# Decay broadcasts of a state-space scan on GpSimd's queue, and an output stage whose scalings come later and whose last two pairs stand in source order

## The chip, the cores and the metric

The kernel runs on one core of a Trainium2 chip. The metric is the device time of one execution in microseconds; runs of the kernel before and of a changed kernel are taken on the same chip. Engines are named as the profile names them: PE is TensorE (PEld its weight loads), DVE is VectorE, ACT is ScalarE, POOL is GpSimd and SP is SyncE; a trailing q (ACTq, SPq) marks what an engine's queue issues, such as a DMA.

## The reference, cut to what matters

One layer of a hybrid decoder: a Mamba-2 state-space branch (SSD) and a gated linear attention branch (GLA) work on the same normalized input, are projected, gated and added; the sum goes through an output matrix, is added to the residual stream, and a final RMSNorm ends it. Sequence 2048 and 16 meta tokens ahead of it, width 1024, float32.

```python
def hybrid_layer(hres, norm_w, w_in, ...):
    u = rmsnorm(hres, norm_w)
    proj = jnp.einsum('bld,dn->bln', u, w_in)
    z, xbc, dt_raw, q, k, v, g_gla, a_lr, merge_g = split_cols(proj, IN_WIDTHS)
    xbc = jax.nn.silu(causal_depthwise_conv(xbc, conv_w, conv_b))
    ...
    y_r, _ = ssd_chunked(xs[:, m:], dt[:, m:], a, bm[:, m:], cm[:, m:], SSD_CHUNK, s_m)
    ...
    o_r, _ = gla_chunked(q[:, m:], k[:, m:], v[:, m:], log_a[:, m:], GLA_CHUNK, st_m)
    ...
    branch_proj = jnp.einsum('blnc,ncd->blnd', branches, w_branch)
    gates = jax.nn.sigmoid(merge_g.reshape(b, l, N_BRANCH, D_MODEL))
    merged = jnp.sum(gates * branch_proj, axis=2)
    return hres + jnp.einsum('bld,de->ble', merged, w_out)

def ssd_chunked(x, dt, a, bmat, cmat, chunk, state0):
    da = (dt * a).reshape(b, nc, chunk, h).transpose(0, 3, 1, 2)
    da_cum = jnp.cumsum(da, axis=-1)
    seg = da_cum[..., :, None] - da_cum[..., None, :]
    decay = jnp.exp(jnp.where(causal, seg, -jnp.inf))
    ...

def reference(x, meta_tokens, ...):
    ...
    return rmsnorm(h, final_norm_w)[:, N_META:]
```

## The kernel before, in words

Every large product is made of float32 pairs: a matrix is split into a high and a low part, and `accum` (L187 to L191) issues three matmuls for each pair, high by high, high by low, low by high.

**First stage (to about 1500 us).** The sequence is cut into four blocks of 512 rows. For each block four groups of the SSD branch and four heads of the GLA branch follow each other: `ssd_proj` and `gla_proj` issue the projections on PE, and at each `yield` a `step()` advances the generators that run beside them, `ssd_scan` and `gla_scan` above all. Projections collect in three PSUM banks `pj`; ACT empties a feature's bank with L491 and L492. The first block has 528 columns, which take two banks a feature; the other blocks have 512 and take one. Weights are split into parts by ACT (L169) and POOL (L170) in the first block, stored, and loaded in parts in the later ones. POOL also makes sums of weights and inputs for the second stage (L82), scales the state (L586), copies the ends of the convolution (L494) and takes powers for the norms (L233, L258).

In `ssd_scan` each of the four 128-row chunks of a group needs its cumulated decays as rows, the same on all partitions: four heads by 128 numbers. `fetch_cb` (L507) loads them from the DRAM tile `cumd` with a broadcast DMA of 256 KB into one of three `cb` buffers; `before(c)` fetches chunk c+1 and then reads chunk c with four activations (L569) into `dm`, exponentiates (L571) and masks on DVE (L572); `after(c)`, one step later, uses `dm` on PE (L581). There are 4 blocks x 4 groups x 4 chunks = 64 such DMAs.

**Second stage.** Gates, both branch projections and the output matrix run as stages of a Strassen-like scheme: each pair n of row blocks takes seven products p of 12 matmuls of 512 columns, in the order `PS = (1, 2, 6, 7, 5, 3, 4)` for two pairs in turn. The products accumulate in three kinds of bank, "a" (`pj`), "b" (`pt`) and "c" (`pc`); after products 1, 6 and 5 ACT copies "a" into a snapshot `sn` (L1010). Four of the seven finish a result: `DONE = {2: (0, 0), 5: (1, 1), 4: (1, 0), 3: (0, 1)}` gives the row block i and the column half t. `total` (L1026) adds snapshot and bank on DVE.

**The output stage** is the last one, with eight pairs. Its `use` (L1080) adds the residual half row `r` on DVE (L1084), squares it on ACT with a row sum (L1090), and when both halves of a row are there, makes the mean on DVE (L1092, L1093), the power -1/2 on POOL (L1094), scales both halves by it and by the norm weight `fns` on DVE (L1097), and hands two stores to the next product, where `flush` issues them on ACT's queue (L1164); the last row's go to SP's (L1215). `fetch` (L1071) loads the residual half row two products ahead on SP's queue into one of eight `io` buffers, which the store of a row frees. `load_a` (L965) loads the m tiles on the same queue, `sum_a` (L974 to L977) adds them on POOL, `prep_a` (L983, L984) splits them on ACT and DVE.

**What sets the order.** In the first stage PE and SP keep the order of the source, in the second SP alone; the order of all other instructions of an engine is set by the program's scheduler, which sorts by source order and by readiness in a simulated timeline. `order` lists all products of the second stage, and the functions in `todo` are run at their places in it: `at(pos, fn)` puts fn behind the product with that number.

Of the kernel before, what the change touches and what calls it, by code (L numbers as in the profile page):

```python
# [7 lines left out]
F32 = mybir.dt.float32  # L8
# [34 lines left out]
def trunk_kernel(ctx: ExitStack, tc: tile.TileContext, xm, xmt, w_feat, w_tok, w_zm, w_br, w_o,  # L43
# [462 lines left out]

    def fetch_cb(o, g, c):  # L507
        cbs[g, c] = cb = mk(spool, [P, 4, P], F32, "cb", bufs=3)
        nc.scalar.dma_start(cb, o.cumd[4 * g:4 * g + 4, c * P:(c + 1) * P].unsqueeze(0).to_broadcast([P, 4, P]))

    def ssd_scan(o, g, feats, zs):
        m0, ci0 = o.m0, o.ci0
# [425 lines left out]
    class Stage:  # L938
# [41 lines left out]
        def prep_a(self, n, p):  # L980
            src = self.a[n][p]
            t = mk(apl, [P, 2, 4, P], F32R, "a")
            nc.scalar.activation(t[:, 0], src, AF.Copy)  # L983
            nc.vector.tensor_tensor(t[:, 1], src, t[:, 0].bitcast(F32), op=ALU.subtract)  # L984
            self.a[n][p] = t

        def product(self, n, p, early=False):
            key, pool, tag = {1: ("a", pj, "pj"), 6: ("a",) * 3, 5: ("a",) * 3, 3: ("a",) * 3, 2: ("c", pc, "pc"),
                              7: ("b", pt, "pt"), 4: ("b",) * 3}[p]
            if p in (1, 2, 7):  # L990
                self.ps[n, key] = bank(pool, tag)
            ps = self.ps[n, key]
            a = self.a[n][p]
            for j in range(4):
                bt = self.b[p, j]
                accum(ps, (a[:, 0, j], a[:, 1, j]), (bt[:, 0], bt[:, 1]), p in (1, 2, 7) and j == 0, j == 3,
                      skip_group_check=True)
            if p in (1, 6, 5):
                if early and p == 6:
                    return  # L1000
                self.snapshot(n, p, early)
            if p in DONE:
                key, sn = {2: ("c", 1), 5: ("b", 5), 4: ("b", 6), 3: ("a", None)}[p]
                self.use(n, *DONE[p], self.ps[n, key], self.snap.get((n, sn)))


        def snapshot(self, n, p, early=False):
# [2 lines left out]
            nc.scalar.activation(sn, self.ps[n, "a"], AF.Copy)  # L1010
            self.snap[n, p] = sn

    DONE = {2: (0, 0), 5: (1, 1), 4: (1, 0), 3: (0, 1)}
    stores = []

# [7 lines left out]
    def total(ps, snap):  # L1023
        if snap is None:
            return ps
        nc.vector.tensor_tensor(snap, snap, ps, op=ALU.add)  # L1026
        return snap
# [38 lines left out]
                         "p (k c) -> p k c", c=P), fetch, use)  # L1066

    def out_stage():
        fns, res, ssq = [], {}, {}

        def fetch(n, i, t):  # L1071
            r0 = (2 * n + i) * P
# [4 lines left out]
                    fns.append(mk(opl, [P, BLK], F32, "br", bufs=5))  # L1077
                    nc.sync.dma_start(fns[hf], fnw[:, hf * BLK:(hf + 1) * BLK].to_broadcast([P, BLK]))

        def use(n, i, t, ps, snap):  # L1080
            r0 = (2 * n + i) * P
            r = res[n, i, t]
            x = total(ps, snap)
            nc.vector.scalar_tensor_tensor(r, x, 0.5, r, op0=ALU.mult, op1=ALU.add)  # L1084
            first = (n, i) not in ssq
            if first:
                ssq[n, i] = mk(spl, [P, 2], F32, "ssf")
            q = ssq[n, i]
            jk = mk(spl, [P, BLK], BF16, "junk", bufs=1)
            nc.scalar.activation(jk, r, AF.Square, accum_out=q[:, t:t + 1])  # L1090
            if not first:
                nc.vector.tensor_tensor(q[:, 0:1], q[:, 0:1], q[:, 1:2], op=ALU.add)  # L1092
                nc.vector.tensor_scalar(q[:, 0:1], q[:, 0:1], 1.0 / D, EPS, op0=ALU.mult, op1=ALU.add)  # L1093
                nc.gpsimd.tensor_tensor(q[:, 0:1], q[:, 0:1], mhalf[:, 0:1], op=ALU.pow)  # L1094
                for hf in range(2):
                    o = res[n, i, hf]
                    nc.vector.scalar_tensor_tensor(o, o, q[:, 0:1], fns[hf], op0=ALU.mult, op1=ALU.mult)  # L1097
                    store(out[r0:r0 + P, hf * BLK:(hf + 1) * BLK], o)

        return Stage("out", ("o",), seq // (2 * P),  # L1100
                     lambda n, i, j: m_left[(2 * n + i) // 4][j][:, :, (2 * n + i) % 4 * P:((2 * n + i) % 4 + 1) * P],
                     fetch, use)

    stages = []
    for s in range(nsb):
        stages += [gate_stage(s), branch_stage(s, 0), branch_stage(s, 1)]
# [2 lines left out]

    PS = (1, 2, 6, 7, 5, 3, 4)
    order, begins = [], []
    for st in stages:
        begins.append(len(order))
        for n in range(0, st.npairs, 2):
            ps = PS if (st, n) != (stages[-1], st.npairs - 2) else PS[:5] + (4, 3)
            order += [(st, n + i, p) for p in ps for i in range(2)]
    NEARLY = 6
    AHEAD, LOAD = 5, 9  # L1120
    todo = {}
# [81 lines left out]
    for n in range(2):  # L1203
        st.snapshot(n, 6)

    with tc.manual_schedule(engines={mybir.EngineType.SP}):
        run(-1)
        for i, (st, n, p) in enumerate(order):
            if i >= NEARLY:
                due, stores[:] = stores[:], []  # L1210
                st.product(n, p)
                flush(due)
            run(i)
        for dst, src in stores:
            nc.sync.dma_start(dst, src)  # L1215


def _layout(inputs):
# [83 lines left out]
```

## Time and profile before

| | before |
|---|---|
| median of 3 runs | 2293.7 us (2292.3 to 2297.49) |
| the profiled execution, its own time | 2293.83 us |
| its span, first to last instruction | 2292.0 us |
| PE busy | 2232.7 us (97%) |
| DVE, ACT, POOL busy | 1549.2, 1180.1, 683.8 us |
| mean granted PE clock | 0.994 |
| broadcasts of `cb`, issued on ACT's queue | 64, of 256.0 KB |

The span is what the profiler saw between the first and the last instruction; the execution's own time is 1.83 us longer. A row of the trace gives the start in us from the span's start, the duration, the engine, the line, the operation, output and inputs by name, and how many were merged (x4); a bracket behind it tells how long the engine had sat idle before it and what released it. A row of the list of waits reads: who waited, for whom, total us, times, longest.

### The profile page before, as it was taken

What the parts mean: (1) busy time and instruction counts of PE and PEld (TensorE: products, weight loads), DVE (VectorE), ACT (ScalarE), POOL (GpSimd) and SP (SyncE); (2) the same over time, 40 slices, a digit from 0 to 9 for tenths busy, and PEclk for the clock granted to TensorE, in tenths of its full rate; (3) what the DMA queues carried; (4) which work ended last, traced back from release to release, by engine and by line L of the source; (5) the groups of instructions that cost most, each with busy time, mean ns of one, the idle gap of its engine ahead of it and who ended that gap; (6) DMA issues with size and microseconds to landing.
All of it is one profiled execution on the core that took longest, in us unless ns stands there. A gap on an engine that the chain in (4) does not pass through costs nothing. (4 is left out here: it accounts for less than half of the span.)

```text
span 2292.0 us, 36448 instructions
## 1 busy us (share of the span) xinstructions
PE 2232.7 (97%) x12641; PEld 1944.7 (85%) x12641; DVE 1549.2 (68%) x2895; ACT 1180.1 (51%) x2726; POOL 683.8 (30%) x681
## 2 busy tenths in 40 slices
PE   7899999999999999999999999899999999999997
PEld 6899989888889988888888898778888888788776
DVE  5677676675666676667667666674678845788766
ACT  4665655465534455544455544454544545454443
POOL 3344433122222122211212100066333274323331
PEclk9999999999999999999999999999999999999999
DMA  8766776667787676877667654466768865787743
GB/s 298 234 208 216 272 258 211 219 205 231 245 270 218 221 225 208 264 256 245 206 220 223 219 185 157 130 216 211 234 224 292 300 226 197 245 278 262 244 145 121
DMA packets 301544, 518.04 MB, mean 226 GB/s; under 512 B 27696, under 2 KB 143664, under 8 KB 301360
## 3 DMA queue, kind: packets, MB, share of 16 engines
q1 hardware_dynamic: 200400, 402.84, 54.4%
q10 hardware_dynamic: 100960, 112.88, 14.2%
q8 instruction: 99, 1.62, 0.3%
q14 instruction: 85, 0.70, 0.1%
HBM read 368.42 MB, written 147.19 MB: 225 GB/s over the span
## 5 line engine op out<-in xcount | busy, mean ns | idle before, releaser
L189 PE MATMUL pj<-ue,whl 128*128 128x264 f32 (+1 forms) x672 | 238.8, 355 | 12.3 <-ACT acc L492 6.3
L191 PE MATMUL pj<-ue,whl 128*128 128x264 f32 (+1 forms) x672 | 232.3, 346 | 0.6 <-DVE tkc L399 0.6
L190 PE MATMUL pj<-ue,whl 128*128 128x264 f32 (+1 forms) x672 | 231.3, 344 | 0.0
L189 PE MATMUL pj<-uo,whl 128*128 128x512 f32 x512 | 206.6, 404 | 0.0
L191 PE MATMUL pj<-uo,whl 128*128 128x512 f32 x512 | 200.1, 391 | 0.0
L190 PE MATMUL pj<-uo,whl 128*128 128x512 f32 x512 | 199.4, 389 | 0.0
L82 POOL TENSOR_TENSOR wr<-wr 128x256 f32<-128x256 f32 x80 | 68.5, 857 | 430.6 <-DMA wr<-u 176.2
L189 PE MATMUL pj<-b,a 128*128 128x512 f32 x480 | 189.4, 396 | 6.6 <-ACT sn L1010 5.8
L191 PE MATMUL pj<-b,a 128*128 128x512 f32 x480 | 188.6, 393 | 0.0
L190 PE MATMUL pj<-b,a 128*128 128x512 f32 x480 | 187.8, 391 | 0.7 <-DVE b L959 0.7
L170 POOL TENSOR_TENSOR whl<-wr,whl 128x512 fp32r<-128x512 f32 (+1 forms) x100 | 134.0, 1347 | 181.0 <-ACT whl L169 132.8
L974 POOL TENSOR_TENSOR as<-ar,ar 128x512 f32<-128x512 f32 x40 | 59.1, 1476 | 396.3 <-DMA ar<-in_w_br 114.2
L496 DVE SCALAR_TENSOR_TENSOR acc<-cin,hcw,acc 128x512 f32<-128x512 f32 (+1 forms) x192 | 154.6, 805 | 28.8 <-ACT acc L492 27.9
L984 DVE TENSOR_TENSOR a<-ar,a 128x512 fp32r<-128x512 f32 x160 | 125.5, 793 | 57.0 <-ACT a L983 55.3
L959 DVE TENSOR_TENSOR b<-br,b 128x512 fp32r<-128x512 f32 x140 | 120.5, 877 | 52.6 <-ACT b L958 50.7
L189 PEld LDWEIGHTS pj<-ue,whl 128*128 128x128 f32 x672 | 128.9, 192 | 29.9 <-ACT acc L492 7.4
L189 PE MATMUL pj<-whl,ue 128*128 128x256 f32 (+1 forms) x496 | 144.1, 291 | 2.1 <-ACT ue L315 2.1
L189 PE MATMUL pj<-whl,uo 128*128 128x256 f32 (+1 forms) x496 | 143.3, 289 | 0.6 <-DMA whl<-k_zm 0.6
L191 PEld LDWEIGHTS pj<-ue,whl 128*128 128x128 f32 x672 | 128.9, 192 | 15.8 <-POOL whl L170 0.9
L191 PE MATMUL pj<-whl,ue 128*128 128x256 f32 (+1 forms) x496 | 140.6, 284 | 1.4 <-DVE ue L317 1.4
L190 PEld LDWEIGHTS pj<-ue,whl 128*128 128x128 f32 x672 | 129.1, 192 | 14.8
L191 PE MATMUL pj<-whl,uo 128*128 128x256 f32 (+1 forms) x496 | 140.8, 284 | 0.0
(308 smaller groups left out, 6535.2 us busy)
## 6 DMA issues: line engine op xcount, KB each, us to landing
whl<-k_s SPq DMA_DIRECT2D x96, 512.0 KB, 4.3
whl<-k_g SPq DMA_DIRECT2D x96, 512.0 KB, 4.2
whl<-k_v SPq DMA_DIRECT2D x48, 512.0 KB, 3.8
whl<-k_z SPq DMA_DIRECT2D x36, 512.0 KB, 3.7
wr<-in_w_feat SPq DMA_DIRECT2D x64, 256.0 KB, 4.4
k_s<-whl SPq DMA_DIRECT2D x32, 512.0 KB, 3.7
cb<-cumd ACTq DMA_DIRECT2D x64, 256.0 KB, 5.7
y<-gg ACTq DMA_DIRECT2D x64, 256.0 KB, 4.4
```

Source lines behind the costliest of these rows:

```text
L82: nc.gpsimd.tensor_tensor(o, x, y, op=ALU.subtract)
L170: nc.gpsimd.tensor_tensor(hl[:, 1], raw, hl[:, 0].bitcast(F32), op=ALU.subtract)
L189: nc.tensor.matmul(ps, sh, mh, start=first, stop=False, **kw)
L190: nc.tensor.matmul(ps, sh, ml, start=False, stop=False, **kw)
L191: nc.tensor.matmul(ps, sl, mh, start=False, stop=last, **kw)
L496: nc.vector.scalar_tensor_tensor(acc, cin[:, k:k + tt], hcw[:, ti, k:k + 1], acc, op0=ALU.mult, op1=ALU.add)
L959: nc.vector.tensor_tensor(t[:, 1], raw, t[:, 0].bitcast(F32), op=ALU.subtract)
L974: nc.gpsimd.tensor_tensor(s1, a21, a22, op=ALU.add)
L984: nc.vector.tensor_tensor(t[:, 1], src, t[:, 0].bitcast(F32), op=ALU.subtract)
```

## The change

Three things change. `fetch_cb` issues its DMA from GpSimd's queue instead of ACT's.

In the output stage, for all row blocks but the last four, the mean and the power (`scale`) are issued one product after the row's last product, and the two scalings and stores (`finish`) three products after it, each of them held behind the newest DVE instruction of the source (`behind`, with `latest` set in `use` and `prep_a`).

The last pairs' products stand in source order on PE too (4, 4, 3, 3 at the end, as the list `out_order` has them), and their rows are finished differently: the snapshot is added to `r` ahead of the product's end; the first half row of the last three is multiplied by the norm weight at once; the last product is computed in two halves of 256 columns, each with its own add and square; and the last scalings are shared between ACT and DVE.

```diff
     def fetch_cb(o, g, c):
         cbs[g, c] = cb = mk(spool, [P, 4, P], F32, "cb", bufs=3)
-        nc.scalar.dma_start(cb, o.cumd[4 * g:4 * g + 4, c * P:(c + 1) * P].unsqueeze(0).to_broadcast([P, 4, P]))
+        nc.gpsimd.dma_start(cb, o.cumd[4 * g:4 * g + 4, c * P:(c + 1) * P].unsqueeze(0).to_broadcast([P, 4, P]))
...
             a = self.a[n][p]
+            if (self, n, p) == order[-1]:
+                for c in (slice(0, HB), slice(HB, BLK)):
+                    for j in range(4):
+                        bt = self.b[p, j]
+                        accum(ps[:, c], (a[:, 0, j], a[:, 1, j]), (bt[:, 0, c], bt[:, 1, c]), False, j == 3,
+                              skip_group_check=True)
+                    self.use(n, *DONE[p], ps, None, c)
+                return
...
-        def use(n, i, t, ps, snap):
-            r0 = (2 * n + i) * P
+        def use(n, i, t, ps, snap, cols=None):
             r = res[n, i, t]
-            x = total(ps, snap)
-            nc.vector.scalar_tensor_tensor(r, x, 0.5, r, op0=ALU.mult, op1=ALU.add)
+            if snap is not None and n >= seq // (2 * P) - 2:
+                nc.vector.scalar_tensor_tensor(r, snap, 0.5, r, op0=ALU.mult, op1=ALU.add)
+            else:
+                ps = total(ps, snap)
...
+            c = cols or slice(0, BLK)
+            k = t + (c.start > 0)
+            latest[:] = [nc.vector.scalar_tensor_tensor(r[:, c], ps[:, c], 0.5, r[:, c], op0=ALU.mult, op1=ALU.add)]
+            nc.scalar.activation(jk[:, c], r[:, c], AF.Square, accum_out=q[:, k:k + 1])
+            row = n, i, t
+            if row == at_once[-1] or (first and (n, i) in [w[:2] for w in at_once[1:]]):
+                if k < 2:
+                    nc.vector.tensor_tensor(r[:, c], r[:, c], fns[t][:, c], op=ALU.mult)
+                if k == 1 and not first:
+                    mean(q)
+                if k == 2:
+                    last = nc.vector.scalar_tensor_tensor(q[:, 0:1], q[:, 2:3], 1.0 / D, q[:, 0:1],
+                                                          op0=ALU.mult, op1=ALU.add)
+                    nc.gpsimd.tensor_tensor(q[:, 0:1], q[:, 0:1], mhalf[:, 0:1], op=ALU.pow)
+                    with tc.issue_after(last.ins):
+                        nc.vector.tensor_tensor(r[:, c], r[:, c], fns[t][:, c], op=ALU.mult)
+                    finish(*row)
+            elif row in at_once:
+                scale(*row)
+                finish(*row)
...
+        def finish(n, i, t):
+            r0 = (2 * n + i) * P
+            q = ssq[n, i][:, 0:1]
+            early, late = res[n, i, 1 - t], res[n, i, t]
+            if (n, i, t) in at_once[1:]:
+                nc.scalar.activation(early, early, AF.Identity, scale=q)
+                if (n, i, t) == at_once[-1]:
+                    nc.vector.tensor_scalar(late, late, q, None, op0=ALU.mult)
+                else:
+                    nc.vector.scalar_tensor_tensor(late, late, q, fns[t], op0=ALU.mult, op1=ALU.mult)
+            else:
+                for o, fn in ((early, fns[1 - t]), (late, fns[t])):
+                    nc.vector.scalar_tensor_tensor(o, o, q, fn, op0=ALU.mult, op1=ALU.mult)
+            for hf, o in ((1 - t, early), (t, late)):
+                store(out[r0:r0 + P, hf * BLK:(hf + 1) * BLK], o)
+
+        def behind(fn, *row):
+            with tc.issue_after(latest[0].ins):
+                fn(*row)
+
+        for i, (n, p) in enumerate(out_order):
+            row = n, *DONE.get(p, (0, 0))
+            if p in (3, 4) and i + 4 < len(out_order):
+                later.append((i + 1, lambda row=row: behind(scale, *row)))
+                later.append((i + 3, lambda row=row: behind(finish, *row)))
+            elif p in (3, 4):
+                at_once.append(row)
...
+    for i, fn in later:
+        at(begins[-1] + i, fn)
...
-    with tc.manual_schedule(engines={mybir.EngineType.SP}):
-        run(-1)
-        for i, (st, n, p) in enumerate(order):
...
+    run_out = ExitStack()
+    run_out.enter_context(tc.manual_schedule(engines={mybir.EngineType.SP}))
+    run(-1)
+    for i, (st, n, p) in enumerate(order):
+        if i == len(order) - 2 * len(PS):
+            run_out.close()
+            run_out.enter_context(tc.manual_schedule(engines={mybir.EngineType.PE, mybir.EngineType.SP}))
```

`scale` and `mean` hold the same DVE and POOL instructions as L1092 to L1094. The row sums `ssf` get eight buffers of three columns instead of four of two.

More of the change, by code (lines that the diff above doesn't have):

```diff
@@ L1011, in snapshot @@
             self.snap[n, p] = sn
+    latest, later, order = [], [], []
     DONE = {2: (0, 0), 5: (1, 1), 4: (1, 0), 3: (0, 1)}
@@ L1085, in use @@
             first = (n, i) not in ssq
             if first:
-                ssq[n, i] = mk(spl, [P, 2], F32, "ssf")
+                ssq[n, i] = mk(spl, [P, 3], F32, "ssf", bufs=8)
             q = ssq[n, i]
             jk = mk(spl, [P, BLK], BF16, "junk", bufs=1)
[L1090 to L1098, printed above, removed]
+            c = cols or slice(0, BLK)
```

38 lines of the change are left out of this document (24 added, 14 removed).

## The prediction

> **What bounds the kernel now.** I read the busy line first, then the idle time of PE stretch by stretch, then the list of PE's waits in the two places that the change touches.
>
> ```profile
> span 2292.0 us, 36448 instructions
> PE 2232.7 (97%) x12641; PEld 1944.7 (85%) x12641; DVE 1549.2 (68%) x2895; ACT 1180.1 (51%) x2726; POOL 683.8 (30%) x681
> ...
> 0.00:100.00 100.00, 80.67 (x557) 76.71 (x558) 55.70 (x111) 56.45 (x130) 36.69 (x40) 0.95 0.83 277
> 400.00:1130.00 730.00, 727.52 (x4466) 648.73 (x4464) 478.74 (x1064) 368.54 (x945) 161.72 (x220) 1.00 0.73 231
> 2250.00:2292.00 42.00, 30.55 (x134) 24.69 (x132) 23.39 (x43) 12.53 (x28) 3.24 (x6) 0.90 0.32 111
> ...
> PE pj L189 <- ACT acc L492: 6.3, 5, 4.2
> ...
> PE pj L189 <- ACT sn L1010: 3.8, 3, 2.4
> ```
>
> PE bounds the whole: it is idle for 59.3 us of 2292.0. No matmul is removed, so the change can only win idle time of PE, or lose some. Idle time lies at the two ends: 19.3 us in the first 100 us and 11.4 in the last 42, against 2.5 us in the 730 from 400 on (the first number after the length of a stretch is PE's busy time). The two waits are those that the change can reach: ACT's late emptying of projection banks in the first block (6.3 us, five times), and ACT's late snapshots in the output stage (3.8 us, three times, between 2130 and the end).
>
> **The decay broadcasts.** All 64 leave ACT's queue for POOL's. On ACT they cost nothing now: 1.26 us are four activations 0.29 apart, so that a group begun at 140.46 hands over at 141.63, with the issue of 0.37 us run beside it.
>
> ```profile
> L509 ACTq DMA_DIRECT2D cb<-cumd x64: 361/377/1278, 58.6 to 1318.2; - x64
>   ACT sq L569: 6.5, 8
> ...
> 140.30 0.37 ACTq L509 DMA_DIRECT2D cb<-cumd  x1
> 140.46 1.26 ACT L569 ACTIVATE sq<-cb,tkc 128x128 f32<-128x128 f32 x4
> 141.63 0.97 ACT L569 ACTIVATE sq<-cb,tkc 128x128 f32<-128x128 f32 x3
> 145.55 1.28 ACT L569 ACTIVATE sq<-cb,tkc 128x128 f32<-128x128 f32 x4 [0.71 <-DMA cb<-cumd]
> 147.61 0.59 PE L189 MATMUL pj<-ue,whl 128*128 128x264 f32 x1 [4.17 <-ACT acc L492]
> 195.87 0.39 PE L189 MATMUL pj<-ue,whl 128*128 128x264 f32 x1 [0.71 <-ACT acc L492]
> 143.93 1.26 POOL L170 TENSOR_TENSOR whl<-wr,whl 128x512 fp32r<-128x512 f32 x1 [3.37 <-issue]
> ```
>
> There are three cb buffers and four chunks a group. So three broadcasts of a group are issued with the group before, long ahead, and only the fourth waits for chunk 0 to be read: issued at 140.30, used at 145.55, with ACT already waiting 0.71 us for it. This fourth one is where lateness shows. In two groups of the first block ACT's next work is L491 and L492, which empty the bank that PE waits for (until 147.61 and 195.87, for 4.17 and 0.71 us). Whatever the fourth broadcast loses there, PE loses.
>
> What a broadcast costs on POOL no row shows, nor how much later it lands. From below: zero, the same landing. From above: one op of POOL to write it out and one POOL op already ahead of it in order, 2 x 1.26 = 2.6 us. I take one such op, 1.3 us, since POOL's software handling of 256 KB is nearest to a POOL op of that size (L170). That gives 2 x 1.3 = +2.6 us. The third group that could feel it (the first, near 87 us) makes the upper end 3 x 2.6 = +7.8. The lower end is a gain: ACT's order is made anew by the program's scheduler, and if L491 and L492 come ahead of the late broadcast's readers in both groups, 4.17 + 0.71 = 4.9 us of waiting go.
>
> [...]
>
> The other three blocks have cover.
>
> ```profile
> 483.60 0.79 ACT L492 ACTIVATE acc<-pj,hcb,hcw 128x512 f32<-128x512 f32 x1
> 498.28 0.72 PE L451 MATMUL pj<-act,w 48*128 48x512 f32 x2
> ```
>
> There a feature fills one bank, not two: the bank freed at 484.39 is next taken by the third allocation after it, at 498.28, 13.9 us later. Cost zero; a broadcast would have to be over 10 us late to show. Behind the broadcasts on POOL stand L170 (first block alone), L82, L586 and the powers; PE's list of waits names POOL nowhere, and each of them would be late by one or two issues. Zero too, with the upper end above as its bound.
>
> **The output stage's stalls.** The chain of the longest of the three:
>
> ```profile
> 2170.30 1.30 POOL L974 TENSOR_TENSOR as<-ar,ar 128x512 f32<-128x512 f32 x1 [5.00 <-DMA ar<-m]
> 2171.55 0.55 POOL L1094 TENSOR_TENSOR ssf<-ssf,mhalf 128x1 f32<-128x1 f32 x1
> 2172.14 3.42 DVE L1097 SCALAR_TENSOR_TENSOR io<-io,ssf,br 128x512 f32<-128x512 f32 x2 [2.86 <-POOL ssf L1094]
> 2173.92 0.34 ACTq L1164 DMA_DIRECT2D out_h<-io  x1
> 2174.31 0.60 ACT L1010 ACTIVATE sn<-pj 128x512 f32<-128x512 f32 x1 [4.82 <-DVE io L1097]
> 2174.96 0.80 PE L189 MATMUL pj<-b,a 128*128 128x512 f32 x1 [2.38 <-ACT sn L1010]
> ...
> DVE io L1097 <- POOL ssf L1094: 14.8, 14, 5.2
> ```
>
> POOL waits for a load, the power stands behind that, DVE's scaling behind the power, ACT's store behind the scaling, the snapshot behind the store, PE behind the snapshot. After the change the power is issued one product later and the scaling three products after the row's last, each held behind the newest DVE instruction. A product of 12 matmuls takes 2.7 us (below), so DVE's scaling has two products, 5.5 us, between it and the power; the longest wait on the power is 5.2. I take all 3.8 us as won. Ends: 0 and -3.8.
>
> What is late next is the row's store, then the io buffer that it frees, then the load into it:
>
> ```profile
> SPq L1074 <- DMA out_h<-io: 55.7, 14, 11.4
> ...
> DVE io L1084 <- DMA io<-in_xm: 7.5, 3, 3.5
> ```
>
> SP already spends 55.7 us on io buffers, with the m loads queued behind them, and DVE waits 7.5 us on late x rows without PE noticing. Nominally three products of delay are 8 us, but scalings now run late anyway, each blocked behind the one before. I count nothing here and keep it as a rival.
>
> **The tail.** From the last matmul's end at 2280.56 to 2292.0 are 11.4 us.
>
> ```profile
> 2272.14 0.39 PE L189 MATMUL pt<-b,a 128*128 128x512 f32 x1
> 2274.66 0.39 PE L191 MATMUL pt<-b,a 128*128 128x512 f32 x1
> 2280.16 0.40 PE L191 MATMUL pj<-b,a 128*128 128x512 f32 x1
> 2281.97 0.63 ACT L1090 ACTIVATE junk<-io 128x512 bf16<-128x512 f32 x1 [4.64 <-DMA out_h<-io]
> 2277.55 0.15 DVE L1093 TENSOR_SCALAR ssf<-ssf 128x1 f32<-128x1 f32 x1
> 2278.46 1.41 DVE L1097 SCALAR_TENSOR_TENSOR io<-io,ssf,br 128x512 f32<-128x512 f32 x2 [0.75 <-POOL ssf L1094]
> 2287.43 1.41 DVE L1097 SCALAR_TENSOR_TENSOR io<-io,ssf,br 128x512 f32<-128x512 f32 x2 [0.73 <-POOL ssf L1094]
> 2288.21 1.00 SPq L1215 DMA_DIRECT2D out_h<-io  x2
> ...
> 482.44 0.42 DVE L592 TENSOR_TENSOR c<-c,pc 128x256 f32<-128x256 f32 x1
> 473.26 0.38 ACT L847 ACTIVATE junk<-pc 128x256 bf16<-128x256 f32 x1
> 473.53 0.20 ACT L847 ACTIVATION_READ_ACCUMULATOR junk<-pc 128x1 f32 x1
> ...
> 1004.22 0.28 PE L190 MATMUL pj<-whl,ue 128*128 128x256 f32 x1
> 1009.60 0.28 PE L191 MATMUL pj<-whl,ue 128*128 128x256 f32 x1
> ```
>
> Now three rows finish behind the last matmul: their squares start at 2281.97, six scalings follow, the last pair ending at 2288.84, and 3.2 us later all is stored. After it, source order on PE gives 4, 4, 3, 3 for the last pairs, so three rows are finished under products, and the last product is cut into two halves of 256 columns. Its matmuls cost nothing extra: from 1004.22 to 1009.60 are 46 steps of 0.117 us, and 24 x 0.117 = 2.8 us, against 12 x 0.229 = 2.7 (from 2272.14 to 2274.66 are 11 steps).
>
> Behind the last matmul stand: add of a half 0.42; square and its accumulator 0.47 (473.26 to 473.73); scale, power and way back 0.9 (2277.55 to 2278.46), beside which DVE's multiply by the norm weight runs hidden; one scaling of 512 columns 0.7 (1.41/2), the other half of the row beside it on ACT; then 3.2 as now, and 0.4 since both stores are ready together and SP issues one after the other (0.5 each); steps between engines 0.1. Sum 6.2. In the way is one scaling of the row before (0.7), which I charge by half: 6.5 us. Ends: 5.8 (no second store behind the first) and 8.0 (that scaling whole, and 1.1 us of wait between the products, since product 4 now follows product 5 directly into the same bank). Gain 11.4 - 6.5 = 4.9, from 3.4 to 5.6.
>
> **Sum.** +2.6 - 3.8 - 4.9 = -6.1 us, a span of 2285.9. The profiled execution took 2293.83 us, 1.8 more than its span and 0.1 above the median of 2293.7; so I forecast 2287.6 us.
>
> **The rivals.**
> A. ACT's new order puts L491 and L492 ahead of the fourth broadcast's readers. For: PE waited from 143.44 on, two us before cb was there, so their bank had long been full. Against: the scheduler chose otherwise with the same instructions. -4.9 instead of +2.6: 2293.7 - 4.9 - 3.8 - 4.9 = 2280.1.
> B. The held rows move the wait: io buffers come free 8 us later, x rows and m loads are late behind each other on SP, DVE waits for x instead of the power, and ACT's stores block snapshots as before. For: 55.7 us of SP's waits. Against: 7.5 us of such waits reach no matmul now. The 3.8 us stay: 2293.7 + 2.6 - 4.9 = 2291.4.
> C. Slower: POOL's issue is dear. Place: the fourth broadcast in three groups of the first block, in front of L491 and L492. Each us of lateness costs 3 us, so it eats the gain of 8.7 from 2.9 us on, and decides the sign. At 5 us (the POOL issue ops of one group in a row, 4 x 1.26): 2293.7 + 15 - 8.7 = 2300.0. For: ACT has no slack there, it waits for this very DMA in 8 places. Against: POOL's ops here are 1.3 us and POOL is 30% busy.
> [...]
> D. The output stage doesn't do what it says: the scheduler still puts other DVE work in front of the last row, so the tail stays at 8 us or more and half the stalls stay: 2293.7 + 2.6 - 1.9 - 3.4 = 2291.0.
>
> **How the numbers follow.** Forecast 0.50, A 0.14, B 0.14, C 0.14, D 0.08. A measurement of this kernel can tell about 0.2% from no change, 4.6 us: faster is below 2289.1, slower above 2298.3. The forecast's own range is 2284.5 to 2290.5 (the ends of the tail and 0.8 to 5 us for the broadcasts), nine tenths of it faster: 0.45; with A 0.14, and a quarter of B and D, 0.06, faster is 0.65. Slower is C beyond 4.4 us of lateness, 0.12. The rest, 0.23, is no change. The range reaches from A's 2280, less 0.7 for the shortest tail, to 2296.5 (B with 7.8 for the broadcasts); beyond lie most of C and little of A, together under 0.2.
>
> **What would show it.** Right: the power of a row no longer directly ahead of its scaling, no PE wait on L1010 after 2130, about 6.5 us from last matmul to the end, and ACT's waits for cb grown by 1 to 2 us each, with PE's two waits on L492 longer by as much. Wrong: a PE wait in the output stage with DVE waiting on io<-in_xm ahead of it (B); POOL issues of over 3 us and PE waits on L492 of 7 us and more (C); L491 ahead of the fourth broadcast's readers in ACT's order (A).

## The result, and the profile after

| | before | changed |
|---|---|---|
| median of 5 runs each | 2293.7 us (2292.3 to 2297.49) | 2283.1 us (2276.93 to 2287.05) |
| ratio to before, 95% interval | | 0.9948 [0.9928, 0.9967] |
| profiled execution, its span | 2293.83, 2292.0 us | 2281.62, 2279.8 us |

The changed kernel is faster by 10.6 us, by the interval by 7.6 to 16.5 us. The forecast was 2287.6 us, 6.1 less than before. One of the twelve executions of the broadcasts alone (below) took 3163.2 us at a granted clock of 0.655; it is left out, and that kernel's median is that of the other eleven. The page of the changed kernel first: the span, PE's busy line, and the queue that now carries the broadcasts (packets, MB, share of the DMA engines' time).

```profile
span 2279.8 us, 36537 instructions
PE 2227.2 (98%) x12653; PEld 1942.9 (85%) x12653; DVE 1565.6 (69%) x2899; ACT 1181.3 (52%) x2731; POOL 731.9 (32%) x745
...
q0 software_dynamic: 5120, 16.78, 2.6%
```

PE is idle for 52.6 us, 6.7 less than before, and busy for 5.5 us less with the same products: matmuls at a lower granted clock count as busy too (in the kernel before PE is busy for all 3.40 us from 2175.00 on, at a clock of 0.55). The busy time can't be put down to the change, though: a second profile of the same changed kernel (below) has 2233.5 us busy and 49.2 idle. The 64 broadcasts now have a queue of their own: 5120 packets, 80 for each. POOL is busy for 48 us more, about the 64 issues at 0.77 us. The same stretches of the changed kernel as before (length, PE, PEld, DVE, ACT, POOL, clock, DMA share, GB/s):

```profile
0.00:100.00 100.00, 79.71 (x552) 75.70 (x553) 57.43 (x111) 57.23 (x133) 42.73 (x48) 0.95 0.82 276
400.00:1130.00 730.00, 725.95 (x4459) 647.26 (x4458) 485.01 (x1063) 367.71 (x945) 187.35 (x252) 1.00 0.73 231
2250.00:2279.80 29.80, 22.37 (x109) 18.49 (x107) 13.86 (x30) 9.96 (x23) 2.31 (x4) 0.96 0.23 85
```

In the start and the middle PE is idle for 1.0 and 1.6 us more than before. Of these stretches only the end gains: after 2250 PE is idle for 7.4 us instead of 11.4. The list of PE's waits in the changed kernel, from 20 to 2280 us:

```profile
PE pj L189 <- ACT acc L492: 5.0, 5, 2.2
...
PE pj L189 <- ACT sn L1018: 2.8, 3, 1.1
```

The longest wait on L492 fell from 4.2 to 2.2 us; the snapshots (now L1018) cost 2.8 us over both stages instead of 5.8, and the longest is 1.1 us instead of 2.4.

**The broadcasts.** The rows of the line that issues them, with the issue's duration (least, median, most, in ns), ACT's wait for them, and the time from issue to landing:

```profile
L509 POOL DMA_DIRECT2D cb<-cumd x64: 747/766/942, 57.0 to 1314.4; - x64
...
  ACT sq L569: 17.0, 11
...
DMA to landing us min/median/max: 3.9/6.0/8.2
```

An issue keeps POOL for 0.77 us, against 0.38 on ACT's queue, and ACT waits 17.0 us for cb instead of 6.5. Yet PE waits less on L492. The group that had the long wait, as the timeline of the changed kernel has it:

```profile
139.58 3.60 ACT L569 ACTIVATE sq<-cb,tkc 128x128 f32<-128x128 f32 x12
143.47 0.75 POOL L509 DMA_DIRECT2D cb<-cumd  x1 [0.41 <-ACT sq L569]
145.33 0.36 ACT L491 ACTIVATE cin<-pj 128x264 f32<-128x264 f32 x1
145.60 0.55 ACT L492 ACTIVATE acc<-pj,hcb,hcw 128x264 f32<-128x264 f32 x1
146.20 0.39 PE L189 MATMUL pj<-ue,whl 128*128 128x264 f32 x1 [2.21 <-ACT acc L492]
148.69 0.40 ACT L569 ACTIVATE sq<-cb,tkc 128x128 f32<-128x128 f32 x1 [0.16 <-DMA cb<-cumd]
```

Before, the four activations of the last chunk stood ahead of L491 and L492, and the bank waited with them for the late broadcast. Now L492 runs at 145.60 and those activations at 148.69, three microseconds behind it. The second of the two groups is turned round in the same way: its L491 starts at 190.13, the late activations at 193.24.

**The output stage.** POOL's timeline in the changed kernel, across the place where the long stall was:

```profile
2156.50 0.56 POOL L1128 TENSOR_TENSOR ssf<-ssf,mhalf 128x1 f32<-128x1 f32 x1 [2.42 <-DVE ssf L1123]
2159.10 0.94 POOL L1128 TENSOR_TENSOR ssf<-ssf,mhalf 128x1 f32<-128x1 f32 x1 [2.05 <-DVE ssf L1123]
2164.28 0.93 POOL L1128 TENSOR_TENSOR ssf<-ssf,mhalf 128x1 f32<-128x1 f32 x1 [4.25 <-DVE ssf L1123]
2167.47 0.55 POOL L1128 TENSOR_TENSOR ssf<-ssf,mhalf 128x1 f32<-128x1 f32 x1 [2.26 <-DVE ssf L1123]
2173.20 1.29 POOL L974 TENSOR_TENSOR as<-ar,ar 128x512 f32<-128x512 f32 x1 [5.17 <-DMA ar<-m]
```

POOL still waits 5.17 us for the load of m (5.00 before), but no power stands behind it: the four of these two pairs are done by 2168.02. DVE's waits for the powers, over the output stage, fell from 14.8 us in 14 to this:

```profile
DVE io L1142 <- POOL ssf L1128: 1.5, 3, 0.7
```

The one wait of PE for a snapshot that is left there has another cause:

```profile
2174.57 1.63 POOL L975 TENSOR_TENSOR as<-as,ar 128x512 f32<-128x512 f32 x1
2174.97 1.79 DVE L1102 SCALAR_TENSOR_TENSOR io<-sn,io 128x512 f32<-128x512 f32 x1
2176.85 0.63 ACT L1103 ACTIVATE junk<-io 128x512 bf16<-128x512 f32 x1 [2.10 <-DVE io L1102]
2178.11 0.50 PE L189 MATMUL pj<-b,a 128*128 128x512 f32 x1 [1.14 <-ACT sn L1018]
```

DVE's add takes 1.79 us beside POOL's sums instead of 0.69, ACT's square waits for it, and the snapshot stands behind the square on ACT. The last section comes back to this add.

**The tail.** Around the last matmul of the changed kernel and behind it (selected rows):

```profile
2271.21 0.38 PE L189 MATMUL pj<-b,a 128*128 128x256 f32 x1 [0.52 <-DVE io L1102]
2272.61 0.28 PE L191 MATMUL pj<-b,a 128*128 128x256 f32 x1
2273.09 0.72 ACT L1135 ACTIVATE io<-io,ssf 128x512 f32<-128x512 f32 x1 [1.18 <-POOL ssf L1128]
2273.71 0.40 ACT L1103 ACTIVATE junk<-io 128x256 bf16<-128x256 f32 x1
2275.17 0.72 ACT L1135 ACTIVATE io<-io,ssf 128x512 f32<-128x512 f32 x1 [0.97 <-POOL ssf L1113]
2275.92 0.82 SPq L1284 DMA_DIRECT2D out_h<-io  x2
```

The last matmul ends at 2272.89, and 6.9 us later all is stored (11.5 before, by 2280.56 and 2292.0). The last row's square waits 0.36 us for the row before it (ACT's L1135 until 2273.81), and from the stores' issue to the end are 3.9 us. The first row of the fence is a wait that was not there before: the second half of the last product writes into the bank that DVE is reading for the first half.

### The profile page after: what moved, and what is told of

It is laid out like the page before. It is cut to its first block, busy times and chain, and to the rows that moved or that the text cites. A ratio compares the mean times of both kernels' runs of the same rounds, so it can differ in the third digit from the quotient of the medians.

```text
span 2279.8 us, 36537 instructions
## 1 busy us (share of the span) xinstructions
PE 2227.2 (98%) x12653; PEld 1942.9 (85%) x12653; DVE 1565.6 (69%) x2899; ACT 1181.3 (52%) x2731; POOL 731.9 (32%) x745
## 3 DMA queue, kind: packets, MB, share of 16 engines
q10 hardware_dynamic: 67168, 96.10, 11.6%
q0 software_dynamic: 5120, 16.78, 2.6%
## 4 chain that ended last, share of the span: by engine, by line
PE 78%; DMA 7%; DVE 7%; ACT 3%; issue 3%; POOL 1%; SPq 0%; ACTq 0%; POOLq 0%; DVEq 0%
PE pj L189 18%; PE pj L191 18%; PE pj L190 18%; PE pt L189 3%; PE pt L190 3%; PE pt L191 3%; PE pc L581 2%; PE pc L191 2%; PE pc L189 2%; PE pc L190 2%; PE pc L732 1%; DMA br<-out_t 1%; DMA acc<-in_xmt 1%; PE pc L582 1%; PE pc L584 1%
## 5 line engine op out<-in xcount | busy, mean ns | idle before, releaser
L189 PE MATMUL pj<-ue,whl 128*128 128x264 f32 (+1 forms) x672 | 238.1, 354 | 11.3 <-ACT acc L492 5.0
L189 PE MATMUL pj<-b,a 128*128 128x512 f32 (+1 forms) x484 | 189.2, 391 | 3.4 <-ACT sn L1018 2.8
L190 PE MATMUL pj<-b,a 128*128 128x512 f32 (+1 forms) x484 | 187.8, 388 | 1.7 <-DVE b L959 1.7
L191 PE MATMUL pj<-b,a 128*128 128x512 f32 (+1 forms) x484 | 188.8, 390 | 0.0
L496 DVE SCALAR_TENSOR_TENSOR acc<-cin,hcw,acc 128x512 f32<-128x512 f32 (+1 forms) x192 | 162.2, 845 | 29.6 <-ACT acc L492 27.3
L974 POOL TENSOR_TENSOR as<-ar,ar 128x512 f32<-128x512 f32 x40 | 57.4, 1436 | 388.8 <-DMA ar<-in_w_br 148.2
L190 PEld LDWEIGHTS pj<-ue,whl 128*128 128x128 f32 x672 | 128.4, 191 | 14.8
```

What stands on the lines that cost most here:

```text
L189: nc.tensor.matmul(ps, sh, mh, start=first, stop=False, **kw)
L190: nc.tensor.matmul(ps, sh, ml, start=False, stop=False, **kw)
L191: nc.tensor.matmul(ps, sl, mh, start=False, stop=last, **kw)
L496: nc.vector.scalar_tensor_tensor(acc, cin[:, k:k + tt], hcw[:, ti, k:k + 1], acc, op0=ALU.mult, op1=ALU.add)
L974: nc.gpsimd.tensor_tensor(s1, a21, a22, op=ALU.add)
```

## The experiments

All are compared with the kernel before on the same chip; its medians there were 2294.17 us (the first four kernels), 2293.75 us (the next four) and 2292.22 us (the last three).

**The parts, one at a time.** Four kernels: the broadcasts alone, both edits of the output stage with the broadcasts back on ACT's queue, the delayed scalings alone, the tail alone.

```diff
# broadcasts alone (in the kernel before)
-        nc.scalar.dma_start(cb, ...)
+        nc.gpsimd.dma_start(cb, ...)
# output stage alone (in the changed kernel)
-        nc.gpsimd.dma_start(cb, ...)
+        nc.scalar.dma_start(cb, ...)
# delays alone: output stage alone, with the tail's branches off and PE's order left to the scheduler
-            if (self, n, p) == order[-1]:
+            if False:
...
-        run_out.enter_context(tc.manual_schedule(engines={mybir.EngineType.PE, mybir.EngineType.SP}))
+        run_out.enter_context(tc.manual_schedule(engines={mybir.EngineType.SP}))
# tail alone: output stage alone, with every scale and finish issued at once, none held
```

> The kernel before with the 64 broadcasts on GpSimd's queue, nothing else changed. Theory 1 (the changed kernel's trace: PE was 2.7 us ahead of the kernel before at its 8000th matmul, about 1277 us, and 3.8 us ahead where the output stage begins): 2.5 to 4 us faster than before, about 2290.5, with PE's wait on L492 near 144 us down from 4.17 to about 2.2 and ACT's L491 ahead of the fourth broadcast's readers. Rival (the recorded forecast): the fourth broadcast lands later in front of L491, 2.6 us slower, about 2296.3. Rival 3: no difference, the 2.7 us are the start of the run alone, 2293.7.

> The changed kernel with the broadcasts back on ACT's queue: the output stage alone. Theory 1: the stage's stalls (3.8 us and the slower matmuls behind the longest of them) and the tail (11.4 to 6.9 us) make 8 to 8.5 us, about 2285.4; PE's first 1300 us as in the kernel before, with 4.2 us of wait at 143 us. Rival: the two parts help each other (another order made for the whole program), and this alone gives less than 6 us, over 2287.7.

> The kernel before with the delayed scalings alone: mean and power one product later, scalings and stores three products later, held behind the newest DVE instruction; the last four rows are finished at once as before, PE's order and the last product are as before, broadcasts on ACT's queue. Theory 1: PE's waits on L1010's snapshots go from 3.8 us to about 1, and the slow matmuls behind the wait of 2.4 us go too: 3.5 to 4.5 us faster, 2289.7, with a tail of 11 us as before. Rival B of the prediction (io buffers come free later, the wait moves to the loads): less than 1 us.

> The kernel before with the new ending alone: last two pairs in source order on PE, last product in halves, shared scalings; all other rows are finished at once as before, broadcasts on ACT's queue. Theory 1: the tail goes from 11.4 to 6.9 us, stalls stay as before: 4.5 us faster, 2289.2. Rival: without the delay the last pairs inherit late scalings of the rows before them, and PE, now bound to source order, waits for them: less than 3 us faster.

| kernel | median | ratio, 95% interval |
|---|---|---|
| broadcasts alone | 2292.00 us | 0.9994 [0.9985, 1.0003] |
| output stage alone | 2283.06 us | 0.9955 [0.9943, 0.9967] |
| delays alone | 2285.91 us | 0.9967 [0.9954, 0.9980] |
| tail alone | 2288.90 us | 0.9981 [0.9973, 0.9990] |

The broadcasts alone change nothing that can be measured (-3.4 to +0.7 us); the output stage alone gives the whole gain. Delays (-7.6 us, -10.6 to -4.6) and tail (-4.4, -6.2 to -2.3) add up to it within their intervals. The delays gained more than the 3.5 to 4.5 us expected; the tail came as expected.

One profile of each shows where. The table is worked out from PE's rows: the first matmul of the output stage (counted back from the last one, 672 matmuls, 684 where the last product is cut in halves), the last matmul's end, the span's end.

| | stage begins | last matmul ends | end | first to last matmul | tail | whole stage |
|---|---|---|---|---|---|---|
| before | 2119.72 | 2280.55 | 2292.04 | 160.8 | 11.5 | 172.3 |
| broadcasts alone | 2113.90 | 2276.91 | 2288.47 | 163.0 | 11.6 | 174.6 |
| delays alone | 2118.77 | 2273.61 | 2284.95 | 154.8 | 11.3 | 166.2 |
| tail alone | 2122.64 | 2285.19 | 2292.01 | 162.6 | 6.8 | 169.4 |
| output stage alone | 2115.94 | 2271.70 | 2278.51 | 155.8 | 6.8 | 162.6 |
| changed | 2115.88 | 2272.89 | 2279.84 | 157.0 | 6.9 | 164.0 |
| changed, profiled again | 2119.65 | 2275.72 | 2282.67 | 156.1 | 6.9 | 163.0 |

The first column is a warning: two profiles of the same changed kernel reach the output stage 3.8 us apart, and three kernels with the first stage of before reach it between 3.8 us earlier and 2.9 us later than before did. So the 3.8 us by which the changed kernel's profile led there say nothing of the broadcasts. The two profiles of the changed kernel differ by 6.3 us in PE's busy time for the same matmuls, as matmuls at half clock take longer (0.43 us apart instead of 0.23 behind the 2.38 us wait of the kernel before, shown below).

The stage's own length repeats better, but not equally well. With the change it took 163.0 and 164.0 us; the stage as it was before took 172.3 and 174.6 in the two first rows, and 170.8, 172.8 and 174.8 in the profiles of three experiments below that also leave it as it was (four buffers, the later broadcast, and the bank emptied first in the kernel before). The delays take 6.0 us out of the matmuls of the kernel before (4.4 to 8.5 against the other four profiles of that stage), the new ending takes 4.5 to 4.7 behind the last matmul.

The flip in ACT's order comes with the broadcasts' queue, not with the output stage. Broadcasts alone, ACT's and PE's timeline:

```profile
144.32 0.55 ACT L492 ACTIVATE acc<-pj,hcb,hcw 128x264 f32<-128x264 f32 x1
144.92 0.39 PE L189 MATMUL pj<-ue,whl 128*128 128x264 f32 x1 [2.21 <-ACT acc L492]
147.93 0.40 ACT L569 ACTIVATE sq<-cb,tkc 128x128 f32<-128x128 f32 x1 [0.67 <-DMA cb<-cumd]
```

**A later broadcast.** On top of the broadcasts alone, the fourth cb buffer of each group is cleared four times on POOL ahead of its DMA.

```diff
+        if c == 3:
+            for _ in range(4):
+                nc.gpsimd.memset(cb, 0.0)
         nc.gpsimd.dma_start(cb, ...)
```

> The kernel before with the broadcasts on GpSimd's queue, and each fourth broadcast held back by four clears of its buffer on GpSimd, an estimated 2 to 5 us of lateness in 16 places. Theory 1 (ACT's new order has L491 ahead of the fourth broadcast's readers, and elsewhere there are 14 us of cover): PE does not notice, within 3 us of the same kernel without the clears (2292.5), while ACT's waits for cb grow by 2 to 5 us each. Rival C of the prediction (each us of lateness in the first block costs PE three): 6 to 15 us slower, 2299 to 2308.

2298.35 us, ratio 1.0019 [1.0009, 1.0030], some 6 us above the broadcasts alone, and the intervals don't overlap: theory 1 (within 3 us) fails. The profiled execution is the fastest of the ten, 2293.43 us, so it shows only part of the loss. PE's waits in it, 20 to 1300 us, and then two rows of ACT:

```profile
PE pj L189 <- ACT acc L492: 6.1, 4, 2.5
...
PE pc L584 <- DVE sq L575: 2.6, 3, 1.8
...
90.50 1.28 ACT L572 ACTIVATE sq<-cb,tkc 128x128 f32<-128x128 f32 x4 [0.73 <-DMA cb<-cumd]
609.65 3.04 ACT L572 ACTIVATE sq<-cb,tkc 128x128 f32<-128x128 f32 x10 [0.40 <-ACT gg L621]
```

Against 4.5 us in 3 for the broadcasts alone, the waits on L492 grow to 6.1 in 4. The longest, 2.5 us at 95.32, comes 5 us behind an activation that waited for its broadcast (90.50); in the same place the broadcasts alone had 2.0 us. PE also waits longer for masked decays (L575 here is L572), 2.6 us instead of 0.5. But the longest of these waits, 1.8 us at 615.20, is not a late broadcast: ACT's activations from 609.65 did not wait for cb, they stand in one block ahead of the exponentials. So the kernel is slower, as rival C had it, but a cost of the lateness itself is not shown: the four clears are 2.1 us of lateness ahead of the DMA, they add 34 us of operations on POOL (64 of 0.53), and they change the order of other work, and this run doesn't separate the three.

**Four buffers.** With a fourth cb buffer no broadcast waits for a reader. The kernel before, with that alone:

```diff
-        cbs[g, c] = cb = mk(spool, [P, 4, P], F32, "cb", bufs=3)
+        cbs[g, c] = cb = mk(spool, [P, 4, P], F32, "cb", bufs=4)
```

> The kernel before, broadcasts on ACT's queue, with four cb buffers instead of three, so that the fourth broadcast of a group is issued as early as the other three. Theory 1 (order, not landing): ACT's waits for cb (6.5 us) go, PE's wait at 143 us falls by the 0.7 us of ACT's wait at most, the time is within 2 us of before, 2292 to 2294. Rival (the fourth broadcast's lateness makes PE's waits there): PE's waits on L492 fall from 6.3 us to under 3, 3 to 5 us faster.

2324.25 us, ratio 1.0131 [1.0116, 1.0145]: 30 us slower; neither expectation had that. ACT waits for cb no more, but PE does for the mask, which was no wait before. PE's longest waits, 20 to 1300 us, then ACT and DVE in one group of the second block, and last, from the kernel before, the first activation and the first exponential of the same group:

```profile
PE pc L581 <- DVE sq L572: 13.0, 7, 2.3
...
476.84 0.40 ACT L569 ACTIVATE sq<-cb,tkc 128x128 f32<-128x128 f32 x1
477.49 1.86 ACT L569 ACTIVATE sq<-cb,tkc 128x128 f32<-128x128 f32 x6
479.25 0.69 ACT L569 ACTIVATE sq<-cb,tkc 128x128 f32<-128x128 f32 x2
479.83 2.16 ACT L569 ACTIVATE sq<-cb,tkc 128x128 f32<-128x128 f32 x7
481.89 0.63 ACT L571 ACTIVATE sq<-sq 128x512 f32<-128x512 f32 x1
482.55 0.73 DVE L572 TENSOR_TENSOR sq<-sq,sq 128x512 f32<-128x512 f32 x1 [2.58 <-ACT sq L571]
...
473.62 0.40 ACT L569 ACTIVATE sq<-cb,tkc 128x128 f32<-128x128 f32 x1
477.49 0.63 ACT L571 ACTIVATE sq<-sq 128x512 f32<-128x512 f32 x1
```

All sixteen activations now stand ahead of the first exponential, from 476.84 to 481.89, 5.1 us. In the kernel before they were twelve, from 473.62 to 477.49, 3.9 us, because the fourth buffer wasn't there. The missing buffer held the scheduler to an order that serves PE better. The 13.0 us of waits are under half of the loss. In the profile PE is idle for 75.6 us instead of 59.3 and busy for 2247.0 instead of 2232.7 with the same matmuls: 16.3 us of idle time and 14.3 of slower matmuls make up the 30.6 us by which the span grew. The slow matmuls go with the new waits: between 400 and 1350 us the kernel before never falls to half clock, and this one does six times for about 3.5 us, near 579, 893, 941, 988, 1258 and 1306, each time within 2 us behind one of the waits for L572.

**The bank emptied first.** In the first block, the activations on cb of chunks 1 to 3 are held on ACT behind the next group's first L492, once in the kernel before, once in the changed one; then the changed kernel and this one side by side.

```diff
-            for h in range(4):
-                nc.scalar.activation(dm[:, h], cb[:, h], AF.Relu, scale=-1.0, ...)
+            hold = emptied.get((o.b, 4 * g + 4)) if m0 and c else None
+            with tc.issue_after(hold.ins) if hold is not None else ExitStack():
+                for h in range(4):
+                    nc.scalar.activation(dm[:, h], cb[:, h], AF.Relu, scale=-1.0, ...)
```

> The kernel before, broadcasts on ACT's queue, and one order forced: in the first block ACT's reads of the broadcasts of chunks 1 to 3 stand behind the emptying of the next group's first feature (L491, L492). Theory 1 (PE's waits of 3.1 us at 82 and 4.2 us at 143 come from ACT's order, chunks read early ahead of a full bank, and not from the broadcast's landing): the wait at 143 falls below 1 us and that at 195 goes, 3 to 6 us faster, about 2289.5. Rival (the late landing makes the wait): the wait at 143 stays above 3 us, since the fourth broadcast lands as before. Rival 2: the wait only moves to the scan's own matmuls (L581) or another bank: within 1.5 us of before.

> The changed kernel with the same forced order in the first block. Theory 1: the two gains add, 2 to 4 us faster than the changed kernel, about 2280.5, as it already has half of the gain at 143 us (its wait there is 2.2 us). Rival: nothing over the changed kernel, 2283.

> The changed kernel itself, beside the next one on the same chip. Theory: 2283 us, ratio to the kernel before 0.994 to 0.997, the output stage's PE waits 2 us or less and the tail 6.9 us.

> The changed kernel with the activations on cb of chunks 1 to 3 of the first block held behind the next group's first L492 on ACT. Theory (the wait that the hold removes is 2.2 us, and what it costs is several waits of 1 us and less): within 2 us of the changed kernel beside it. Rival (the halved clock behind the wait goes with it): 3 us or more below the changed kernel beside it, with intervals that do not overlap.

| kernel | median | ratio, 95% interval |
|---|---|---|
| before, held | 2291.89 us | 0.9992 [0.9982, 1.0001] |
| changed, held | 2280.58 us | 0.9945 [0.9932, 0.9958] |
| changed, again | 2284.09 us | 0.9962 [0.9950, 0.9974] |
| changed, held, again | 2279.76 us | 0.9947 [0.9935, 0.9959] |

In the kernel before the hold changes nothing that can be measured, close to what the second rival said: the 4.2 us wait goes, and seven of up to 1.5 us (5.4 in all) take its place. On top of the change the medians are 2.5 and 4.3 us lower, and ten runs lie within 2278.38 and 2283.47 us, eleven of the changed kernel within 2276.93 and 2287.05. The intervals still overlap (0.9950 to 0.9959), so neither theory of the last expectation holds outright: a gain of 2 to 4 us is likely, not shown. In the profiles of the last two rows PE is idle for nearly the same time, 49.2 and 48.5 us, but busy for 2233.5 and 2229.3: a gain would lie in the clock behind the waits more than in the waits, but the busy time of two profiles of one kernel differed by more than that (6.3 us). It is the best version tried.

**The halves.** The changed kernel with its last product whole, and add, square and multiply behind it still in halves.

```diff
-                for c in (slice(0, HB), slice(HB, BLK)):
-                    for j in range(4):
-                        ...
-                    self.use(n, *DONE[p], ps, None, c)
+                for j in range(4):
+                    ...
+                for c in (slice(0, HB), slice(HB, BLK)):
+                    self.use(n, *DONE[p], ps, None, c)
```

> The changed kernel with its last product computed whole (12 matmuls of 512 columns, one group a line) while the add, the square and the norm multiply behind it stay cut into halves. Theory (the halves let the first half be added, squared and multiplied under the second half's matmuls): behind the last matmul stand one more add of 256 columns (0.42) and one more multiply or square of 256 columns (0.4), so 6.9 us from the last matmul to the end become 7.5 to 7.9; in return PE's wait of 0.5 us between the halves on L1102 goes, so the last matmul ends 0.4 to 0.6 earlier: the time changes by +0.1 to +0.5 us, which the interval will not tell from nothing. Rival (the halves carry the tail's gain): a tail of 9 us or more and 2 us or more on the time.

2284.08 us, ratio 0.9963 [0.9951, 0.9975], beside 2284.09 for the changed kernel. Its tail is 7.95 us instead of 6.95, its matmuls from the output stage's first to the last take 154.9 us instead of 156.1 and 157.0. What the halves win behind the last matmul they lose ahead of it, as the theory had it.

## Why the prediction was right, and which terms were off

The direction, the place of the gain and two mechanisms held; the size was short by 4.5 us, from three terms. The two large errors, on the broadcasts and on the stalls, point the same way.

**Bound.** That PE bounds the whole, and that only its idle time can be won, held. Of the two waits and the tail named there, the wait on L492 gave nothing that can be measured; the whole gain came out of the snapshots' wait and the tail.

**Broadcasts, +2.6 us forecast, -1.4 us measured (-3.4 to +0.7): the term that failed.** The price was near enough. For lateness the prediction took one POOL op of 1.26 us; the issue takes 0.39 us longer (0.77 against 0.38) and the way from issue to landing 0.3 us longer (6.0 against 5.7), at most 0.7 us in all. What failed is the step that multiplied it by two groups "in front of L491 and L492". That holds for ACT's old order alone. With the broadcasts on POOL's queue the scheduler put L491 and L492 ahead of the late readers in both groups, which is rival A's mechanism; at the second group, near 196 us, no wait is left. Of A's 4.9 us about 2.7 can be seen in these two waits (4.17 to 2.21, and 0.71 to none), 1.3 in all waits on L492, and in the time none is shown. The expected "PE's waits longer by as much" was wrong; the growth of ACT's waits for cb came (6.5 to 17.0 us), nine of the eleven in the three later blocks, where PE has the cover that the prediction named.

**Rival C** did not come: issues of 0.77 us are far below its threshold. Held back on purpose, the fourth broadcast goes with a loss of some 6 us, whose cause that run leaves open. With DVE busy for 69% of the span the 64 issues took 747 to 942 ns, and the slowest landing took 8.2 us against 7.9 before.

**Stalls, -3.8 us forecast, -6.0 us in the trace of the delays alone and -7.6 us in its time: mis-sized.** The mechanism is the one predicted, a power behind a POOL op that waits for a load. But the forecast counted only the wait, as its upper end. The longest of PE's waits there also cost what followed it. Windows of the kernel before, around the 2.38 us wait (the granted clock is the number behind POOL's busy time):

```profile
2172.50:2175.00 2.50, 0.12 (x2) 0.04 (x1) 2.50 (x2) 0.69 (x2) 2.50 (x2) 0.93 0.73 240
2175.00:2178.40 3.40, 3.40 (x9) 2.69 (x10) 2.92 (x7) 1.05 (x2) 0.96 (x2) 0.55 0.51 176
2178.40:2185.00 6.60, 6.60 (x30) 5.38 (x29) 4.70 (x7) 3.84 (x9) 1.62 (x1) 1.00 0.27 97
```

Behind the wait the clock is 0.55 for 3.4 us, and matmuls come 0.43 us apart instead of 0.23: some 1.5 us more. 3.8 and 1.5 are 5.3 of the 6.0 us. The other four profiles of that stage agree: less the waits for snapshots its matmuls take 157.1 and 157.4 us where the clock was halved once, and 155.8 and 156.1 where it was not (157.0 in the kernel before, 154.8 with the delays alone, which have no wait). In the changed kernel's own profile a wait of 1.1 us on L1018 is left, and the delays take less there.

**Tail, -4.9 us forecast, -4.5 us measured, less what the halves cost.** It was forecast as 6.5 us and is 6.9; the stores take 3.9 us instead of 3.6. What the prediction counted at nearly nothing was the split: it costs the 0.52 us wait between the halves in one bank, and 0.9 to 1.2 us in the matmuls in all (155.8 and 156.1 against 154.9), so the split wins nothing. The gain is then that of the last rows' order and of the shared scalings; which of them brings how much was not tried.

**Signs.** Of the four things that would show it right, the tail was there, and the wait on the snapshots nearly: the sign said none after 2130, and one of 1.1 us is left (none with the delays alone). ACT's waits for cb grew as said, PE's on L492 did not. The power ahead of its scaling was half wrong: the third and fourth row of each four still scale right behind their power (2164.28, then 2165.25), and it does no harm, because the power no longer stands behind L974. **Rival B** did not come: DVE waits 6.0 us for x rows (7.5 before) and SP 52.5 us for buffers that stores free (55.7 before), and PE's only wait for a snapshot there is the one of 1.1 us shown above, behind a slow add. **Rival D** neither.

**The range.** The forecast's own range, 2284.5 to 2290.5, does not come out of the ends it names: +0.8 - 3.8 - 5.6 and +5 - 3.8 - 3.4 on 2293.7 give 2285.1 and 2291.5. No run shows the 0.8 us in it; the runs show at most 0.7 us of lateness for one broadcast, and -3.4 to +0.7 us in the time. The measured 2283.1 lies below either, in the wider range. That this one held is partly luck: its lower end was opened for A's gain on the broadcasts, and the gain came from the stalls.

## What to carry to other kernels

Here a late transfer cost what stood behind its reader on the reader's engine: with ACT's waits for cb up from 6.5 to 17.0 us, PE's on L492 fell from 6.3 to 5.0, as L492 no longer stood behind the late readers. So a queue change is priced by the order that the scheduler makes afterwards, not by the old one; check whether the order flips before multiplying a delay by the places it used to hit. A stall of PE can be worth more than its length, because the clock may be halved behind it (here 0.55 for 3.4 us behind a wait of 2.38 us, some 1.5 us more): look at the granted clock there. And two profiles of one kernel can differ by several us ahead of the place of interest (3.8 us here): compare a stage by its own length, from its first matmul to its end, and in more than one profile.

## What the hardware showed that was not expected

**A PE wait of 2 us and more is mostly followed by half clock, but not always.** In the thirteen profiles here, from 20 us on, 22 waits of PE lasted 2.38 us or more: behind 21 of them the granted clock was 0.5 at once or within 2 us, for some 3.4 us or longer. Of ten waits between 2.0 and 2.3 us it followed seven. And one wait, for L810 near 1485 us (1517 with four buffers), lasts 1.93 us in every profile: half clock follows in seven, none in six. Behind 4.17 us in the kernel before (first row) and 3.76 us in the broadcasts alone (second row) it was halved. Behind 2.21 us in the changed kernel (third row) it was not, and behind the same 2.21 us in the second profile of the same kernel (fourth row) it was. The one long wait without it is 3.47 us in the tail alone (fifth row).

```profile
147.60:151.00 3.40, 3.39 (x17) 3.39 (x18) 2.60 (x3) 2.89 (x6) 1.48 (x2) 0.56 1.02 360
...
2171.40:2174.80 3.40, 3.37 (x8) 2.67 (x9) 2.92 (x7) 1.12 (x2) 1.03 (x2) 0.53 0.50 176
...
146.20:149.60 3.40, 3.40 (x28) 3.40 (x29) 3.36 (x5) 3.24 (x9) 2.06 (x2) 1.00 0.94 309
...
146.87:150.27 3.40, 3.40 (x15) 3.40 (x16) 3.36 (x5) 2.96 (x8) 2.05 (x2) 0.50 0.95 289
...
2179.00:2182.40 3.40, 3.38 (x15) 2.79 (x16) 2.92 (x7) 1.12 (x2) 1.02 (x2) 1.00 0.49 167
```

Rows three and four are one kernel and one place with the same wait, so the wait's length alone does not decide; what else does is not shown. These stretches are also where the two profiles of the changed kernel part: at 147 and at 1487 us the second runs at half clock and the first does not.

**A DVE operation with two inputs in SBUF, beside POOL, took over twice as long; with one input in PSUM it did not.** In the changed kernel the same add took 0.69 us with POOL idle (first row) and 1.79 us beside POOL's sums (2174.97, in the section on the output stage). An add with one input in a PSUM bank (`pt`), wholly under a POOL sum, took 0.68:

```profile
2169.39 0.69 DVE L1102 SCALAR_TENSOR_TENSOR io<-sn,io 128x512 f32<-128x512 f32 x1
...
2223.18 1.75 POOL L977 TENSOR_TENSOR as<-ar,as 128x512 f32<-128x512 f32 x1
2223.69 0.68 DVE L1035 TENSOR_TENSOR sn<-sn,pt 128x512 f32<-128x512 f32 x1
```

Thirteen operations of the first kind start under a POOL sum in this output stage. Each ends 0.54 to 0.56 us behind the end of that sum (2174.97 and 1.79 give 2176.76, the sum ended at 2176.20), so what sets their time is how much of the sum is left when they start. In the kernel before, two scalings beside POOL's sums took 3.42 us against 1.41 with POOL idle (2172.14 and 2278.46, in the prediction), and ended 0.55 us behind the end of a sum, at 2175.56 and 2175.01.
